# Seven products for the seventh up block, weight sums that are additions and partly accumulating transfers, and down chunks over two blocks

## The chip, the cores and the metric

One core of one Trainium2 chip. The metric is the device time of one execution in microseconds (us), the median of several runs. Everything else that is quoted comes from one profiled execution of the kernel before, so sums are made against that execution's own time.

Engines are named as the profile names them: PE (TensorE) multiplies, PEld is its weight load, DVE (VectorE) and ACT (ScalarE) do elementwise work, POOL (GpSimd) does little in this kernel, and SP (SyncE) issues the loads from memory.

## The reference

Two decoder layers over 256 tokens of width 2048. Each layer has an attention, a cross attention into 256 memory tokens, and an MLP, each behind an RMS norm and added to the residual. All of the change lies in the MLP:

```python
def sq_relu_mlp(h, wup, wdown):
    return jnp.square(jax.nn.relu(h @ wup)) @ wdown

# per layer, with D_MODEL = 2048 and D_FF = 8192
x = x + sq_relu_mlp(rms_norm(x, mlp_norm[i]), mlp_wup[i], mlp_wdown[i])
```

All numbers are float32.

## The kernel before

**Precision.** A weight tile arrives as float32 (`raw`, 128 x 2048, 1 MB) and is split into two float32r tiles: `whi` (a cast, on ACT) and `wlo = raw - whi` (a subtraction, on DVE). Activations are split the same way into a `unit`. A product is then three matmuls: hi x hi, hi x lo, lo x hi.

**Jobs and buffers.** A *job* is one weight tile: one load (issued by SP), and two half splits (`split_pieces`: each half is one ACT cast of 128 x 1024 and one DVE subtraction of the same size). There are six `raw` buffers (`RAWS = 6`), and four buffers each for `whi` and `wlo`, so splits can be two jobs ahead of PE and no more. `fill` issues the loads of jobs ahead of their use. PE runs in program order; the order of the other engines' instructions is chosen by the scheduler when the kernel is built, and each of them is then in order.

**The MLP.** The 8192 hidden columns are cut into eight blocks of 1024, each of two halves of 512. The tokens are two tiles `t` of 128. A plain up block (`Chunk`, kind `"up"`) is eight jobs of 24 matmuls. A `Seven` block computes the same by seven products instead of eight (a Strassen/Winograd scheme over two token tiles, two halves of K, two halves of the columns): products `p1` to `p7`, each as two jobs `x = 0, 1` of 12 matmuls. The activation sums `s1` to `s4` are formed once per layer (`Forms`). The weight sums are made by DVE on the raw tiles before they are split: `p5`, `p7`, `p6` and `p4` each load one more tile, and combine it with the raw tile of an earlier product (line 766, two instructions per job). The products are then combined by DVE into four hidden tiles (line 794, seven instructions per block), which ACT squares after a relu, PE transposes and ACT and DVE split again.

Six of the eight blocks (`SEVEN = (1, 2, 3, 5, 6, 7)`) are done so; blocks 0 and 4 are plain. A down chunk (`Chunk`, kind `"down"`) accumulates 512 of the 2048 output columns over one or one and a half blocks in two PSUM banks, one per token tile, and is then added to the residual by DVE (line 439).

**Order.** `mlp_line` writes the order of a layer's jobs by hand-made costs: `vector` says what a job costs DVE, `tensor` what it costs PE; a `lead` decides whether the next job is taken from the Seven blocks or from the rest (the other up halves and the down chunks).

Most matmuls and casts are recorded on the line of a helper (155 for a matmul, 193 and 194 for the splits), so groups are read by their tile names: `pr` are the products of the Seven blocks, `mm` all other products, `ax` the transposes and the attention's tiles.

Of the kernel before, what the change touches and what calls it, by code (L numbers as in the profile page):

```python
# [17 lines left out]
P = 128  # L18
# [27 lines left out]
def trunk(ctx, tc, x, xT, mem, memT, positions, gcols, gfinal, lam_vecs, consts, W, out):  # L46
# [16 lines left out]
    def nm(s):  # L63
        serial[0] += 1
        return f"{s}_{serial[0]}"
# [81 lines left out]
    def give_back():  # L147
        free_banks[0] += 1

    def mmul(o, stationary, moving, start, stop):  # L150
        n = 1
        for d in moving.shape[1:]:
            n *= d
        clock[0] += max(0.11, n / 2400 + 0.0133)
        return nc.tensor.matmul(o, stationary, moving, start=start, stop=stop)  # L155

    def flip(o, src):
        clock[0] += 0.109
# [209 lines left out]
    class Forms(Stream):  # L368

        def __init__(self, gcol):
            super().__init__(gcol)
            self.raw = [raw_tile().rearrange("p (k t) -> p k t", t=P) for _ in range(NT)]
# [28 lines left out]
        def sums(self):  # L403
            for key in [(t, h) for t in range(NT) for h in range(2)]:
                for task in self.forms[key].tasks:
                    yield task
            for x in range(2):
                a11, a12, a21, a22 = (self.raw[t][:, 8 * h + 4 * x : 8 * h + 4 * x + 4] for t in range(NT) for h in range(2))
                for key, o, p, q, op in (
                    ("s1", a22, a21, a22, ALU.add), ("s3", a21, a11, a21, ALU.subtract),  # L410
                    ("s2", a22, a22, a11, ALU.subtract), ("s4", a12, a12, a22, ALU.subtract),
                ):
                    nc.vector.tensor_tensor(o, p, q, op)
                    self.halves(key, x, o)
                yield T_TURN
# [308 lines left out]
    class Seven:  # L724


        ORDER = ("p1", "p5"), ("p3", "p7", "p6", "p2", "p4")
        A = {"p1": (0, 0), "p2": (0, 1), "p3": "s4", "p4": (1, 1), "p5": "s1", "p6": "s2", "p7": "s3"}

        def __init__(self, l, b):  # L730
            self.l, self.b = l, b
            self.raw = {}
            self.banks = {}

        def fetch(self, i, j, x):
            raw = raw_tile()
            load(raw, W[f"mlp_wup{self.l}"][4 * (2 * self.b + j) + 2 * i + x])
            return raw

        def job(self, p, x):  # L740
            def run():
                r = self.raw
                other = None
                if p == "p1":
                    r["11"] = o = self.fetch(0, 0, x)
                elif p == "p5":
                    o = self.fetch(0, 1, x)
                    other, args = r.pop("11"), lambda a, b: (a, b, ALU.subtract)
                elif p == "p3":
                    r["22"] = o = self.fetch(1, 1, x)  # L750
                elif p == "p7":
                    r["t3"] = o = self.fetch(0, 1, x)
                    other, args = r.pop("22"), lambda a, b: (b, a, ALU.subtract)
                elif p == "p6":
                    r["t2"] = o = self.fetch(0, 0, x)
                    other, args = r.pop("t3"), lambda a, b: (b, a, ALU.add)
                elif p == "p2":
                    r["21"] = o = self.fetch(1, 0, x)
                else:
                    o = r.pop("t2")  # L760
                    other, args = r.pop("21"), lambda a, b: (a, b, ALU.subtract)
                split = split_pieces(o, 4 * CH, 2)
                for h in range(2):
                    if other is not None:
                        half = slice(2 * h * CH, 2 * (h + 1) * CH)
                        nc.vector.tensor_tensor(o[:, half], *args(o[:, half], other[:, half]))  # L766
                    split.next()
                return split.halves

            return run  # L770

        def items(self):
            return [Item(self, (p, x), [self.job(p, x)]) for group in self.ORDER for x in range(2) for p in group]

        def products(self, a, u, copied, out):
            p, x = u
            form = a.form(self.A[p])
            need(form.tasks)
            if x == 0:
                self.banks[p] = bank("pr")  # L780
            o = self.banks[p]
            for h, (hi, lo) in enumerate(take()):
                for k in range(2):
                    kk = 4 * x + 2 * h + k
                    wh, wl = (w[:, k * CH : (k + 1) * CH] for w in (hi, lo))
                    mmul(o, form[:, 0, kk], wh, kk == 0, False)
                    mmul(o, form[:, 0, kk], wl, False, False)
                    mmul(o, form[:, 1, kk], wh, False, kk == 7)
                pump()
            if x == 0:  # L790
                return

            def add(o, p, q, op=ALU.add):
                nc.vector.tensor_tensor(o, p, q, op)

            c, b = copied, self.banks
            if p in ("p1", "p5"):
                c[p] = work.tile([P, CH], F32, tag="ev", name=nm(p), bufs=EVS)
                nc.scalar.copy(c[p], o)
            elif p == "p6":  # L800
                u2, c12 = (work.tile([P, CH], F32, tag="ev", name=nm("u"), bufs=EVS) for _ in range(2))
                add(u2, b["p6"], c["p1"])
                add(c["p5"], u2, c["p5"])
                add(c12, b["p3"], c["p5"])
                out(0, 1, c12)
                add(c["p5"], b["p7"], c["p5"])
                out(1, 1, c["p5"])
                add(u2, b["p7"], u2)
                c["u3"] = u2
            elif p == "p2":  # L810
                add(c["p1"], b["p2"], c["p1"])
                out(0, 0, c["p1"])
            elif p == "p4":
                add(c["u3"], c["u3"], b["p4"], ALU.subtract)
                out(1, 0, c["u3"])

    def mlp_line(l):

# [2 lines left out]
        def up(b, h):  # L821
            return Chunk(l, "up", [(b, h)]).items()

        def down(*halves):
            return [i for c in range(4) for i in Chunk(l, "down", halves, c).items()]

        def both(b):
            return (b, 0), (b, 1)

        line = up(0, 0) + up(0, 1)  # L830
# [12 lines left out]

        def tensor(item):
# [6 lines left out]
        lead, now = 0.0, 0  # L851
        while rest or seven:
            of = rest[0].of if rest else None
            late = rest and of.kind == "down" and any(usable.get(h, math.inf) > now for h in of.halves)
# [5 lines left out]
            if item.of.__class__ is Seven:  # L860
                usable.update({(item.of.b, h): now + 6 for h in range(2)} if item.u == ("p4", 1) else {})
            elif item.of.kind == "up" and item.u == 3:
                usable[item.of.halves[0]] = now + 4
        return line + after, down(*both(7))

    mlp_lines = {l: mlp_line(l) for l in range(2)}

# [193 lines left out]
    def mlp(l, norm, gnext):  # L1061
# [1 line left out]
        rstd = keep2(norm.rstd, 1.0, "r1")  # L1063
        hid = {}

        chunk = {}
        copied = {}

        def out(b, c, t, src, r, wait):
# [31 lines left out]
        def run(line, nxt=None):  # L1101
            for item in line:
                of = item.of
                if isinstance(of, Seven):
                    of.products(
                        a, item.u, copied,
                        lambda t, c, r, b=of.b: out(b, c, t, r, r, T_SQ + 7.0),
                    )
                    continue
                n = len(of.all)  # L1110
# [2 lines left out]
                        finish_chunk(of, matmul_chunk(acts_of(of), turns=True), nxt)  # L1113
                    continue
                if item.u == 0:
                    chunk["ps"] = [bank("mm") for _ in range(NT)]
                    chunk["acts"] = acts_of(of)
                act = chunk["acts"][item.u]
                need(act.tasks)
                for h, (hi, lo) in enumerate(take()):  # L1120
                    for t in range(NT):
                        unit_part(chunk["ps"][t], act, h, hi, lo, t, item.u == 0, item.u == n - 1)
                if item.u == n - 1:
                    finish_chunk(of, chunk["ps"], nxt)

        line, end = mlp_lines[l]
        limit = free_banks[0] - 1
# [274 lines left out]
```

## Time and profile before

| what | value |
|---|---|
| runs, median (lowest to highest of 3) | 2261.57 us (2261.05 to 2264.02) |
| profiled execution, span | 2260.9 us, 0.7 us under the median |
| granted PE clock | 0.999 |
| PE busy | 2236.6 us, 99% of the span |
| DVE busy | 1764.3 us, 78% |
| ACT busy | 1337.3 us, 59% |
| POOL busy | 104.5 us, 5% |
| loads | 475.71 MB, mean 210 GB/s |
| first to last product of the Seven blocks, layer 0 | 545.6 to 1123.4 us |
| the same, layer 1 | 1608.2 to 2185.5 us |

The span runs from the first to the last instruction. Durations of matmuls overlap (one lasts 0.39 us and the next starts 0.227 us after it), so PE counts as busy in gaps of up to 0.16 us. Waits are put down to the event that came last.

### The profile page before, as it was taken

The numbers are of one execution on the slowest core, as the hardware profiler recorded it, in microseconds if no ns is written. First come the engines' busy times: TensorE is split into PE (matmuls) and PEld (weight loads), VectorE is DVE, ScalarE is ACT, GpSimd is POOL, SyncE is SP. The second block draws the span as 40 slices with busy tenths as digits, with TensorE's granted clock in tenths as the row PEclk, the third lists the DMA queues.
The fourth block names the chain that finished last, engine by engine and source line by source line (L and its number), as shares of the span: only waits on it lengthen the run. The fifth ranks groups of instructions, "written<-read, shape, count | busy, mean of one in ns | idle before, by whom it ended". The sixth has DMA issues, their size and how long they took to land.

```text
span 2260.9 us, 27589 instructions
## 1 busy us (share of the span) xinstructions
PE 2236.6 (99%) x10569; PEld 1862.3 (82%) x10569; DVE 1764.3 (78%) x2002; ACT 1337.3 (59%) x1787; POOL 104.5 (5%) x194
## 2 busy tenths in 40 slices
PE   9999999999999999999999999999999999999998
PEld 7888888888888888888889888888888888888886
DVE  6665647778889989888865766778788998888975
ACT  7554546666565665656645655656666656566554
POOL 0201010000000000000000311000000000000001
PEclk9999999999999999999999999999999999999999
DMA  9446555436666667666745334744766676666662
GB/s 362 168 141 214 201 181 208 156 131 235 249 238 227 249 236 259 231 234 223 259 160 184 106 140 149 251 140 149 259 225 241 230 272 222 243 227 246 253 243 75
DMA packets 72564, 475.71 MB, mean 210 GB/s; under 512 B 8304, under 2 KB 8688, under 8 KB 17904
## 3 DMA queue, kind: packets, MB, share of 16 engines
q1 hardware_dynamic: 71856, 472.90, 58.9%
q8 instruction: 83, 1.36, 0.2%
q10 hardware_dynamic: 576, 1.05, 0.2%
q14 instruction: 49, 0.40, 0.1%
HBM read 471.82 MB, written 2.10 MB: 210 GB/s over the span
## 4 chain that ended last, share of the span: by engine, by line
PE 87%; DVE 6%; DMA 4%; issue 1%; ACT 1%; ACTq 0%; DVEq 0%; POOLq 0%
PE mm L155 67%; PE pr L155 14%; DMA raw<-in_mlp_wup_dram 4%; DVE wlo L194 3%; PE ax L155 3%; DVE raw L766 2%; PE ax L159 2%; PE mm L159 1%; ACT whi L193 1%; DMA raw<-in_da_wqkv_dram 0%; DVE x L439 0%; DVE unit L316 0%; DVE unit L488 0%; DVE os L659 0%; DVE unit L289 0%
## 5 line engine op out<-in xcount | busy, mean ns | idle before, releaser
L155 PE MATMUL mm<-whi,unit 128*128 128x512 f32 (+2 forms) x4800 | 1516.4, 389 | 1.3 <-ACT unit L572 0.9
L193 ACT CAST whi<-raw 128x1024 fp32r<-128x1024 f32 (+3 forms) x938 | 976.6, 1041 | 789.4 <-PE mm L155 647.2
L194 DVE TENSOR_TENSOR wlo<-raw,whi 128x1024 fp32r<-128x1024 f32 (+3 forms) x938 | 1124.0, 1211 | 382.8 <-ACT whi L193 366.5
L155 PEld LDWEIGHTS mm<-whi,unit 128*128 128x128 f32 x4800 | 897.8, 188 | 179.0 <-ACT unit L572 1.3
L155 PE MATMUL mm<-wlo,unit 128*128 128x512 f32 (+2 forms) x2400 | 927.7, 387 | 3.9 <-DVE wlo L194 3.7
L155 PEld LDWEIGHTS mm<-wlo,unit 128*128 128x128 f32 x2400 | 451.8, 188 | 90.8 <-DVE wlo L194 7.7
L155 PE MATMUL pr<-whi,unit 128*128 128x512 f32 x1344 | 432.7, 391 | 0.0
L155 PEld LDWEIGHTS pr<-whi,unit 128*128 128x128 f32 x1344 | 252.6, 188 | 51.5
L155 PE MATMUL pr<-wlo,unit 128*128 128x512 f32 x672 | 263.5, 392 | 7.1 <-DVE wlo L194 6.9
L766 DVE TENSOR_TENSOR raw<-raw,raw 128x1024 f32<-128x1024 f32 x192 | 227.7, 1221 | 22.5 <-DMA raw<-in_mlp_wup_dram 22.1
L155 PEld LDWEIGHTS pr<-wlo,unit 128*128 128x128 f32 x672 | 126.3, 188 | 38.1 <-DVE wlo L194 13.0
L439 DVE TENSOR_TENSOR x<-x,mm 128x512 f32<-128x512 f32 x192 | 127.4, 682 | 13.4 <-PE mm L155 12.9
L328 POOL TENSOR_TENSOR rs<-rs,mhalf 128x1 f32<-128x1 f32 (+1 forms) x28 | 23.5, 843 | 1275.2 <-DVE rs L327 1275.2
L288 ACT CAST unit<-ax 128x512 fp32r<-128x512 f32 (+1 forms) x88 | 48.6, 564 | 18.7 <-PE ax L159 16.3
L289 DVE TENSOR_TENSOR unit<-ax,unit 128x512 fp32r<-128x512 f32 (+1 forms) x88 | 57.4, 661 | 2.1 <-ACT unit L288 1.8
L501 ACT ACTIVATE p<-ax,nmax 128x256 f32<-128x256 f32 (+1 forms) x80 | 33.6, 428 | 30.0 <-DVE nmax L499 29.5
L322 ACT ACTIVATE junk<-x 128x512 bf16<-128x512 f32 x56 | 35.1, 627 | 9.4 <-DVE x L439 8.4
L1300 POOL TENSOR_TENSOR x<-x,unit 128x512 f32<-128x512 f32 x6 | 8.9, 1501 | 665.4 <-ACT junk L322 665.4
L155 PE MATMUL ax<-unit,unit 128*128 128x256 f32 (+1 forms) x240 | 37.2, 281 | 0.0
L155 PEld LDWEIGHTS ax<-unit,unit 128*128 128x128 f32 x240 | 34.4, 190 | 2.5
L155 PE MATMUL ax<-raw,unit 128*128 128x256 f32 (+1 forms) x240 | 35.3, 279 | 0.8 <-ACT unit L487 0.6
L155 PEld LDWEIGHTS ax<-raw,unit 128*128 128x128 f32 x240 | 32.0, 191 | 2.4 <-ACT unit L487 1.0
(141 smaller groups left out, 924.4 us busy)
## 6 DMA issues: line engine op xcount, KB each, us to landing
raw<-in_mlp_wup_dram SPq DMA_DIRECT2D x176, 1024.0 KB, 4.9
raw<-in_mlp_wdown_dram SPq DMA_DIRECT2D x128, 1024.0 KB, 5.0
raw<-in_da_wqkv_dram SPq DMA_DIRECT2D x45, 1024.0 KB, 5.1
raw<-in_da_wo_dram SPq DMA_DIRECT2D x16, 1024.0 KB, 5.0
raw<-in_ca_wkv_dram SPq DMA_DIRECT2D x16, 1024.0 KB, 5.0
raw<-in_mla_wo_dram SPq DMA_DIRECT2D x16, 1024.0 KB, 5.2
raw<-in_ca_wq_dram SPq DMA_DIRECT2D x8, 1024.0 KB, 5.0
raw<-in_ca_wo_dram SPq DMA_DIRECT2D x8, 1024.0 KB, 5.0
```

Of the source, the lines that this page charges most:

```text
L155: return nc.tensor.matmul(o, stationary, moving, start=start, stop=stop)
L159: nc.tensor.transpose(o, src, ident)
L193: nc.scalar.copy(hi, r)
L194: nc.vector.tensor_tensor(lo, r, f32(hi), ALU.subtract)
L288: nc.scalar.copy(hi, src)
L289: nc.vector.tensor_tensor(dst[:, 1, :n, t * P : (t + 1) * P], src, f32(hi), ALU.subtract)
L322: nc.scalar.activation(junk[:, : src.shape[1]], src, AF.Square, accum_out=acc)
L328: nc.gpsimd.tensor_tensor(r[:, :n], r[:, :n], mhalf.broadcast_to([P, n]), ALU.pow)
L439: nc.vector.tensor_tensor(xc, xc, ps, ALU.add)
L501: nc.scalar.activation(pr[:, i * w : (i + 1) * w], sb[:, i * w : (i + 1) * w], AF.Exp, bias=nmax[:, i : i + 1], accum_out=ssum[:, i : i + 1],)
L766: nc.vector.tensor_tensor(o[:, half], *args(o[:, half], other[:, half]))
L1300: nc.gpsimd.tensor_tensor(xs[t][:, cc], xs[t][:, cc], gf[:, cc], ALU.mult)
```

## The change

- `SEVEN` gains block 4, so seven blocks go by seven products and block 0 alone is plain.
- The signs of the activation sums are turned (`s1` and `s4`), so that each weight sum is a sum: `p5` uses `p1`'s tile plus one, `p7` uses `p3`'s plus one, `p6` uses `p7`'s plus one, `p4` uses `p6`'s plus one (`SUM`: the product before, the sum's name, the tile that is added).
- A sum whose name is in `ADDED[l]` is no longer made by DVE. After the tile's last half split, POOL issues a transfer that adds the next tile from memory onto the raw tile in place (`accum_op=ALU.add`), and the next product splits that tile. In layer 0 this holds for `t2` (`p7` to `p6`); in layer 1 for `t3`, `t2` and `t4` (`p3` to `p7` to `p6` to `p4`). `t1` stays with DVE in both.
- The products' order is `p1, p5, p2, p3, p7, p6, p4`, both jobs of one product behind each other. `p2` is accumulated onto `p1`'s bank and `p3` onto `p5`'s, after a copy of `p1` and `p5` has been taken, so five DVE instructions combine a block instead of seven.
- A down chunk covers two blocks where it can: its two banks stay open from one block to the next, and there are 18 chunks per layer instead of 28.
- The order's cost of a job no longer counts a sum that a transfer makes, so in layer 1 the jobs of a block stand closer together.

```diff
-SEVEN = (1, 2, 3, 5, 6, 7)
+SEVEN = (1, 2, 3, 4, 5, 6, 7)
+ADDED = ("t2",), ("t3", "t2", "t4")
...
-                    ("s1", a22, a21, a22, ALU.add), ("s3", a21, a11, a21, ALU.subtract),
-                    ("s2", a22, a22, a11, ALU.subtract), ("s4", a12, a12, a22, ALU.subtract),
+                    ("s1", a22, a21, a22, ALU.subtract), ("s3", a21, a11, a21, ALU.subtract),
+                    ("s2", a22, a22, a11, ALU.subtract), ("s4", a12, a12, a22, ALU.add),
...
-        ORDER = ("p1", "p5"), ("p3", "p7", "p6", "p2", "p4")
+        ORDER = "p1", "p5", "p2", "p3", "p7", "p6", "p4"
+        B = {"p1": (0, 0), "p2": (1, 0), "p3": (1, 1)}
+        SUM = {"p5": ("p1", "t1", (0, 1)), "p7": ("p3", "t3", (0, 1)), "p6": ("p7", "t2", (0, 0)), "p4": ("p6", "t4", (1, 0))}
+        AFTER = {before: p for p, (before, _, _) in SUM.items()}
...
+                if p in self.B:
+                    o = self.fetch(*self.B[p], x)
                 else:
-                    o = r.pop("t2")
-                    other, args = r.pop("21"), lambda a, b: (a, b, ALU.subtract)
+                    before, name, block = self.SUM[p]
+                    if name in self.added:
+                        o = self.raw.pop((before, x))
+                    else:
+                        o, other = self.fetch(*block, x), self.raw.pop((before, x))
                 split = split_pieces(o, 4 * CH, 2)
                 for h in range(2):
                     if other is not None:
                         half = slice(2 * h * CH, 2 * (h + 1) * CH)
-                        nc.vector.tensor_tensor(o[:, half], *args(o[:, half], other[:, half]))
+                        nc.vector.tensor_tensor(o[:, half], o[:, half], other[:, half], ALU.add)
                     split.next()
+                if p in self.AFTER:
+                    self.raw[p, x] = o
+                    _, name, block = self.SUM[self.AFTER[p]]
+                    if name in self.added:
+                        add = nc.gpsimd.dma_start(o, self.source(*block, x), accum_op=ALU.add)
+                        tc.keep_in_program_order(add)
...
+            onto = {"p2": "p1", "p3": "p5"}.get(p)
             if x == 0:
-                self.banks[p] = bank("pr")
+                self.banks[p] = self.banks[onto] if onto else bank("pr")
...
-        rest = (
-            up(4, 0) + down(*both(0)) + down(*both(1), (4, 0)) + up(4, 1) + down(*both(2))
-            + down(*both(3), (4, 1)) + down(*both(5)) + down(*both(6))
-        )
+        def down(b):
+            shut, begun = ((0, 1), (2, 3)) if b % 2 else ((2, 3), (0, 1))
+            line = []
+            for c in shut:
+                line += opened.pop(c)[2:] if c in opened else Chunk(l, "down", both(b), c).items()
+            for c in begun:
+                if b == MLP_BLOCKS - 1:
+                    line += Chunk(l, "down", both(b), c).items()
+                else:
+                    opened[c] = Chunk(l, "down", both(b) + both(b + 1), c).items()
+                    line += opened[c][:2]
+            return line
...
-                return 2 + 2 * (p in ("p5", "p7", "p6", "p4")) + x * {"p6": 4, "p2": 2, "p4": 2}.get(p, 0) * 0.55
+                summed = p in Seven.SUM and Seven.SUM[p][1] not in ADDED[l]
+                return 2 + 2 * summed + x * {"p6": 4, "p4": 2, "p2": 1}.get(p, 0) * 0.55
```

The order that `mlp_line` gives in layer 1, with `d` for a down job (24 matmuls): blocks 1 and 2 run `p2x0 p2x1 d p3x0 p3x1 p7x0 p7x1 p6x0 p6x1 d d d p4x0 p4x1`, blocks 3, 4 and 5 `p2x0 p2x1 d p3x0 p3x1 p7x0 p7x1 p6x0 d p6x1 d d p4x0 d p4x1`, blocks 6 and 7 `p2x0 d p2x1 p3x0 p3x1 p7x0 p7x1 d p6x0 p6x1 d d d p4x0 p4x1`. In layer 0 it is, for block 2, `p2x0 p2x1 p3x0 p3x1 p7x0 d p7x1 d p6x0 p6x1 d p4x0 d p4x1`.

DVE in layer 1, block 5, before the change, from the split of `p5`'s second job onward. `raw_15992` is `p3`'s tile, `raw_16016` `p7`'s and `raw_16042` `p6`'s; the sums (L766) stand ahead of splits (L194) of jobs that PE needs earlier:

```order
L766 TENSOR_TENSOR raw_16016<-raw_15992,raw_16016 128x1024 [waits DMAHW7_49,DMAHW0_49,DVE_49]
L766 TENSOR_TENSOR raw_16016<-raw_15992,raw_16016 128x1024
L194 TENSOR_TENSOR wlo_15912<-raw_15903,whi_15911 128x1024 [waits Activation_49]
L194 TENSOR_TENSOR wlo_15950<-raw_15947,whi_15949 128x1024 [waits DMAHW5_49,Activation_49]
L194 TENSOR_TENSOR wlo_15954<-raw_15947,whi_15953 128x1024 [waits Activation_49]
L766 TENSOR_TENSOR raw_16042<-raw_16016,raw_16042 128x1024 [waits DMAHW1_49,DVE_49]
L766 TENSOR_TENSOR raw_16042<-raw_16016,raw_16042 128x1024 [waits DVE_49]
L194 TENSOR_TENSOR wlo_15973<-raw_15970,whi_15972 128x1024 [waits DMAHW6_49,Activation_49]
L194 TENSOR_TENSOR wlo_15977<-raw_15970,whi_15976 128x1024 [waits Activation_49]
L194 TENSOR_TENSOR wlo_15995<-raw_15992,whi_15994 128x1024 [waits Activation_49]
```

The same place after the change (layer 1, block 5, from `p3`'s first job): `raw_16287` is the tile of `x = 0` and `raw_16322` that of `x = 1`, each split in turn as `p3`, `p7` and `p6`:

```order
L195 TENSOR_TENSOR wlo_16290<-raw_16287,whi_16289 128x1024 [waits DMAHW1_49,Activation_49]
L195 TENSOR_TENSOR wlo_16294<-raw_16287,whi_16293 128x1024 [waits Activation_49]
L195 TENSOR_TENSOR wlo_16325<-raw_16322,whi_16324 128x1024 [waits DMAHW2_49,Activation_49]
L195 TENSOR_TENSOR wlo_16329<-raw_16322,whi_16328 128x1024 [waits Activation_49]
L195 TENSOR_TENSOR wlo_16346<-raw_16287,whi_16345 128x1024 [waits DMASW6_49,Activation_49]
L195 TENSOR_TENSOR wlo_16350<-raw_16287,whi_16349 128x1024 [waits Activation_49]
L290 TENSOR_TENSOR unit_16367<-ax_16462,unit_16367 128x4x128 [waits Activation_49]
L195 TENSOR_TENSOR wlo_16371<-raw_16322,whi_16370 128x1024 [waits DMASW7_49,Activation_49]
L195 TENSOR_TENSOR wlo_16375<-raw_16322,whi_16374 128x1024 [waits Activation_49]
L195 TENSOR_TENSOR wlo_16404<-raw_16287,whi_16403 128x1024 [waits DMASW0_49,Activation_49]
L195 TENSOR_TENSOR wlo_16408<-raw_16287,whi_16407 128x1024 [waits Activation_49]
```

The sums are gone from this stretch. Each third and fifth pair of splits waits for an accumulating transfer (`DMASW`) onto the tile that the pair two jobs earlier has read.

POOL in the same block after the change (before it, POOL has nothing in this stretch); each row waits for DVE's last split of the same tile, and the other semaphores name older transfers:

```order
L768 DMA raw_16287<-in_mlp_wup_dram 128x2048 [waits DMAHW1_49,DMAHW3_49,DMAHW0_49,DMAHW6_49,DMASW6_49,DVE_49]
L768 DMA raw_16322<-in_mlp_wup_dram 128x2048 [waits DMAHW2_49,DMAHW4_49,DMASW5_49,DVE_49]
L768 DMA raw_16287<-in_mlp_wup_dram 128x2048 [waits DMASW6_49,DVE_49]
L768 DMA raw_16322<-in_mlp_wup_dram 128x2048 [waits DMASW7_49,DVE_49]
L768 DMA raw_16287<-in_mlp_wup_dram 128x2048 [waits DMASW0_49,DVE_49]
L768 DMA raw_16322<-in_mlp_wup_dram 128x2048 [waits DMASW1_49,DVE_49]
```

Six transfers per block now stand on POOL, in the order `t3`, `t2`, `t4`, each for `x = 0` and then `x = 1`.

More of the change, by code (lines that the diff above doesn't have):

```diff
@@ L154, in mmul @@
         clock[0] += max(0.11, n / 2400 + 0.0133)
-        return nc.tensor.matmul(o, stationary, moving, start=start, stop=stop)
+        return nc.tensor.matmul(o, stationary, moving, start=start, stop=stop, skip_group_check=not alone)
     def flip(o, src):
@@ L853, in mlp_line @@
             of = rest[0].of if rest else None
-            late = rest and of.kind == "down" and any(usable.get(h, math.inf) > now for h in of.halves)
+            late = rest and of.kind == "down" and usable.get(of.halves[rest[0].u], math.inf) > now
             take_seven = seven and (not rest or late or lead <= 0)
@@ L1064, in mlp @@
         hid = {}
-        chunk = {}
         copied = {}
```

94 lines of the change are left out of this document (44 added, 50 removed).

## Prediction

> **What bounds the kernel now.** I read the busy shares first, then the shares of the chain that ended last, then the two MLP stretches apart.
>
> ```profile
> span 2260.9 us, 27589 instructions
> PE 2236.6 (99%) x10569; PEld 1862.3 (82%) x10569; DVE 1764.3 (78%) x2002; ACT 1337.3 (59%) x1787; POOL 104.5 (5%) x194
> PE 87%; DVE 6%; DMA 4%; issue 1%; ACT 1%; ACTq 0%; DVEq 0%; POOLq 0%
> ```
>
> PE is busy nearly throughout, but the chain runs 6% over DVE and 4% over loads, so some of PE's time is waiting that overlapping matmul records hide. To find it I price PE's work from two pieces of the chain without a wait, and hold this against the stretches. The columns after the stretch and its length are the busy time and count of PE, PEld, DVE, ACT and POOL, then clock, DMA share and GB/s; the third row is line 159 alone (PE, PEld), the transposes in layer 0.
>
> ```profile
> 569.93 5.44 PE pr L155 x24
> 641.68 0.44 PE ax L159 x4
> ...
> 545.60:1123.40 577.80, 572.12 (x2561) 469.58 (x2560) 510.66 (x492) 356.52 (x385) 0.00 (x0) 1.00 0.67 239
> 1608.20:2185.50 577.30, 571.97 (x2560) 469.47 (x2559) 510.60 (x492) 356.49 (x385) 0.00 (x0) 1.00 0.68 240
> ...
> 545.60:1123.40 577.80, 16.80 (x112) 13.81 (x112) 1.00 0.67 239
> ```
>
> A matmul takes 5.44 / 24 = 0.2267 us. Layer 0's stretch holds 2561 - 112 = 2449 matmuls, 555.2 us, and 112 / 4 groups of transposes, 12.3 us: 567.5 of 577.8. So 10.3 us are lost there, about 10 in layer 1, 20 together. A piece of the chain shows how (start, length, engine, tile):
>
> ```profile
> 649.00 1.06 ACT whi L193
> 650.09 1.24 DVE wlo L194
> 651.34 4.92 DMA raw<-in_mlp_wup_dram
> 656.34 0.13 DVE raw L766
> 657.49 1.22 DVE raw L766
> 658.70 1.15 DVE wlo L194
> 659.89 1.42 PE pr L155 x5
> ...
> DVE raw L766 <- DMA raw<-in_mlp_wup_dram: 22.1, 27, 2.0
> PEld pr L155 <- DVE wlo L194: 13.0, 14, 1.3
> ```
>
> A weight sum (L766) stands in DVE's order ahead of a split that PE needs sooner, and waits for its own load. DVE so waits 22.1 us in 27 places, and PE's products 13.0 us behind DVE.
>
> **The change, part by part.**
>
> *Matmuls.* A block by products is 14 jobs of 12 matmuls, 168; plain, 8 jobs of 24, 192. One block per layer: 48 fewer, 48 x 0.2267 = 10.9 us less. PE sets the end and nothing covers this, so it is a gain of 10.9.
>
> *DVE and ACT.* The rows:
>
> ```profile
> L193 ACT CAST whi<-raw 128x1024 fp32r<-128x1024 f32 (+3 forms) x938 | 976.6, 1041 | 789.4 <-PE mm L155 647.2
> L194 DVE TENSOR_TENSOR wlo<-raw,whi 128x1024 fp32r<-128x1024 f32 (+3 forms) x938 | 1124.0, 1211 | 382.8 <-ACT whi L193 366.5
> L766 DVE TENSOR_TENSOR raw<-raw,raw 128x1024 f32<-128x1024 f32 x192 | 227.7, 1221 | 22.5 <-DMA raw<-in_mlp_wup_dram 22.1
> L439 DVE TENSOR_TENSOR x<-x,mm 128x512 f32<-128x512 f32 x192 | 127.4, 682 | 13.4 <-PE mm L155 12.9
> L794 DVE TENSOR_TENSOR u<-pr,p 128x512 f32<-128x512 f32 x24 | 16.5, 687 | 0.2
> ```
>
> Sums per layer go from 96 to 84 (layer 0: 7 blocks x 6 x 2) and to 28 (layer 1: 7 x 2 x 2): 12 and 68 times 227.7 / 192 = 1.19 us, 14 and 81 less. Combining takes 7 x 5 = 35 instructions instead of 6 x 7 = 42: 7 x 0.69 = 5 less. Residual adds fall from 56 to 36: 20 x 127.4 / 192 = 13 less. Block 4 has 14 jobs instead of 8, so 12 more half splits: 12 x 1.2 = 14 more on DVE, 12 x 1.04 = 12 more on ACT. DVE gets 18 us lighter in layer 0 and 85 in layer 1. ACT, 357 of 577 us busy, covers its 12. Both engines mostly wait for PE (ACT's idle 789.4 is 647.2 behind `mm`), so this by itself moves the end by nothing.
>
> *The lost 20 us.* They hang on sums ahead of splits, so I scale them with the sums left: 84 / 96 leaves 9.0 of 10.3 in layer 0, 28 / 96 leaves 3 of 10 in layer 1, a gain of 8.4. Fewer instructions on DVE help splits that are merely late, so I take 11 (3 and 8). Bounds: 0, the sums left do the same harm; 20, all goes.
>
> *Banks.* Chunks over two blocks keep four of PE's eight banks open. I find no wait for a bank but this one, and adds become fewer: nothing, and less than 1 us either way.
>
> ```profile
> PEld mm L155 <- DVE x L439: 1.0, 4, 0.3
> ```
>
> *Accumulating transfers.* No row before shows one. POOL is empty in both stretches (0.00 x0 above), so they queue behind nothing there, and the older semaphores that they name belong to loads long landed. They begin when DVE's last split of the tile is done, which PE's buffers time, so they cannot be issued early. ACT's split of the next product waits for their landing; its later splits and casts are queued behind that wait, then DVE's, then PE.
>
> In layer 0 only `p7` to `p6` is so made, with down jobs between; by the order of block 2, at least 9.5 us lie between last split and need. Hidden: 0, up to a transfer of 9.5 us.
>
> In layer 1 the transfers form a chain: `p3` split, transfer, `p7` split, transfer, `p6` split, two jobs (2.7 us each) apart. Splits may be two jobs ahead of PE. Take T = 0 as the end of `p2x1` in blocks 3 to 5. PE's order, with a down job 5.44 and the others 12 matmuls, 2.72, is: d to 5.44, `p3x0` 8.16, `p3x1` 10.88, `p7x0` 13.60, `p7x1` 16.32, then `p6x0`, whose first low half is used at 16.5. A split starts within 0.3 us of PE's freeing the buffer:
>
> ```profile
> 848.11 1.05 ACT L193 CAST whi<-raw 128x1024 fp32r<-128x1024 f32 x1 [0.30 <-PE pr L155]
> ```
>
> The second half of `p3x0` is split by 0.2 + 1.05 + 1.24 = 2.5. With L from issue to landing, `t3` lands at 2.5 + L. A whole split takes 1.05 + 2 x 1.24 = 3.5: `p7x0` is done at 6.0 + L, `t2` lands at 6.0 + 2L, and the first half of `p6x0` (2.3) is ready at 8.3 + 2L. Needed at 16.5: PE waits 2L - 8.2 per block. The same count gives 2L - 5.5 for blocks 1 and 2, which have no down job ahead of `p6x1` (13.7 + 2L against 19.2), and the greater of L - 3.6 and 2L - 10.9 for blocks 6 and 7, which have one ahead of `p6x0`. For L between 4.3 and 7.3 the seven blocks add up to 2(2L - 5.5) + 3(2L - 8.2) + 2(L - 3.6) = 12L - 42.8.
>
> L from the rows:
>
> ```profile
> raw<-in_mlp_wup_dram SPq DMA_DIRECT2D x176, 1024.0 KB, 4.9
> q1 hardware_dynamic: 71856, 472.90, 58.9%
> 1571.00:2261.00 690.00, 675.85 (x3025) 555.16 (x3023) 581.95 (x573) 410.72 (x456) 10.73 (x9) 1.00 0.64 227
> ```
>
> The lower bound is a plain load of the same tile, 4.9: a wait of 16 us. The upper is two loads behind one another, since the transfer takes in two tiles, one from memory and one from the buffer: 9.8, 80 us by the stalls of that length. A 1 MB transfer occupies the 16 DMA engines for 0.589 x 2260.9 x 1.0486 / 472.9 = 2.95 us, so a second pass over the tile adds at least that if it is not overlapped: 4.9 + 2.95 = 7.9. A little of it should overlap, so I take 7.4: 12 x 7.4 - 42.8 = 46 us.
>
> [...]
>
> SP's loads of `p7`, `p6`, `p4` become POOL's in layer 1, so two of the six raw buffers are held from `p3` to `p4`, and the other four carry the rest. A job of 5.44 us still covers a load of 4.9: 0. If that cover goes, PE waits for loads, first at `mm`.
>
> **The sum.** 2260.9 - 10.9 - 11 + 46 = 2285, and 0.7 from span to median: 2286. Its own range: L of 6.0 (29 us) to 8.7 (63 us) gives 2269 to 2303.
>
> **The rivals.**
>
> *Faster: the transfers land like loads.* With L = 4.9 the waits are 16, and with relief of 11 the time is 2256; with the waits gone and the 20 us recovered, 2231. Its middle is 2244. It decides at 12L - 42.8 = 21.9, so L = 5.4. For it: DMA is 0.68 busy in the stretch, so there is room. Against: a second operand must be read.
>
> [...]
>
> *Much slower: the transfers crowd the DMA engines.* Layer 1's last stage moves 152 loads, 152 x 2.95 = 448 of 690 us, 0.65, as the 0.64 above. Now it moves 170, of which 42 count twice: 212 x 2.95 = 625, 0.91. Then L is 9.8 or more, and loads fall late as well: 2260.9 - 21.9 + 80 = 2319. Against: it is still under 1.
>
> *The sums left stand ahead of splits as before,* so that only the waits move: relief 0, 11 us onto each case, 2297 with my L. The transfers do then what the change says, and DVE's lighter load buys nothing. One in five, within the others.
>
> **Chances.** A measurement of this kernel tells about 0.2% (4.5 us) from no change. My forecast 0.42; transfers like loads 0.38; between them, L of 5.0 to 5.8, within 0.2%, 0.07; crowded engines 0.13. So faster 0.38, same 0.07, slower 0.55. The range runs from 2236, which leaves out the best third of the fast case, to 2312, short of the crowded one. The least certain number is L: the rows bound it by a factor of two and its sign turns inside.
>
> **What will show it.** Matmul records of the MLP fall by 48. In layer 1, ACT's `whi` or DVE's `wlo` wait for `raw` from POOL's transfers, some 28 times, and PE's products behind them; POOL's issue rows give L directly. Layer 1's stretch should be some 46 - 8 - 5.4 = 33 us longer than 577.3, layer 0's 3 + 5.4 = 8 shorter than 577.8. If layer 1 is the shorter, L is under 5.4 and my chain is wrong; if PE waits at `mm` for loads, the crowding is right; if DVE's sums still wait 20 us, the relief is.

## The result, and the profile after

The changed kernel takes 2361.62 us (median of 4 runs, 2358.34 to 2365.3) beside 2262.26 of before: a ratio of 1.0441, interval 1.0426 to 1.0455. It is 4.4% slower. The forecast of 2286 had the direction and a quarter of the size, and its range ended at 2312.

The page of the changed kernel, with the parts that answer to those shown of before: span, busy time by engine, shares of the chain that ended last, DMA queues, and loads of one tile with the median time to landing.

```profile
span 2358.1 us, 27600 instructions
PE 2266.0 (96%) x10521; PEld 1872.3 (79%) x10521; DVE 1671.7 (71%) x1892; ACT 1357.4 (58%) x1815; POOL 153.8 (7%) x250
q1 hardware_dynamic: 68976, 451.92, 53.2%
q0 software_dynamic: 8064, 58.72, 13.3%
PE 72%; DMA 12%; DVE 8%; issue 5%; ACT 2%; ACTq 0%; POOLq 0%; DVEq 0%
raw<-in_mlp_wup_dram SPq DMA_DIRECT2D x156, 1024.0 KB, 5.1
raw<-in_mlp_wup_dram POOLq DMA_DIRECT2D x56, 1024.0 KB, 9.4
```

PE issues 48 instructions fewer (10569 to 10521), as forecast, and DVE is 93 us lighter. The chain nevertheless holds 12% of transfers where it held 4%. The 56 accumulating transfers land after 9.4 us, near the upper bound of 9.8 that was taken from two loads. SP's loads still land in 5.1 in the median; those in flight beside the transfers do not, as layer 0 shows below.

The stretches from the first to the last product of the Seven blocks, layer 0 and layer 1 (columns as before: PE, PEld, DVE, ACT, POOL, then granted clock, DMA share, GB/s):

```profile
522.10:1155.90 633.80, 603.98 (x2645) 493.75 (x2645) 512.66 (x487) 381.72 (x416) 12.44 (x14) 0.97 0.77 259
1617.50:2288.40 670.90, 621.81 (x2669) 498.53 (x2668) 457.00 (x432) 379.95 (x417) 36.94 (x42) 0.97 0.84 246
```

The granted clock has fallen from 1.00 to 0.97 in both. To compare kernels whose stretches hold different jobs, I take each PE instruction's distance to the next beyond what it needs (0.227 us for a matmul of 512 columns), and split the sum: "slow" where the matmul itself runs longer than at a granted clock of 1.00 (0.39 us for those 512 columns), "idle" the rest. "Lost" is the sum of the two. Both are in us, for one profiled execution of each kernel, in the stretches of the two layers:

| kernel | span | layer 0: idle + slow | layer 1: idle + slow |
|---|---|---|---|
| before | 2260.9 | 10.3 + 1.3 | 9.9 + 1.3 |
| changed | 2358.1 | 37.5 + 12.5 | 65.2 + 16.4 |
| none: no transfers | 2254.8 | 13.4 + 1.5 | 12.1 + 1.4 |
| plain: transfers that do not add | 2277.8 | 14.4 + 1.9 | 29.8 + 3.9 |
| pin: all DVE sums late | 2395.8 | 60.1 + 22.0 | 63.8 + 21.1 |
| soft3: sums three jobs back | 2337.5 | 29.0 + 4.7 | 59.5 + 16.0 |
| nonesoft3: the same without transfers | 2281.3 | 23.9 + 2.9 | 23.8 + 2.9 |
| t2t4: one sum more by transfer in layer 0 | 2338.4 | 22.1 + 3.4 | 65.2 + 20.4 |
| spaced: layer 1 in another order | 2304.8 | 34.3 + 13.3 | 25.6 + 3.7 |
| warm: PE kept busy in layer 0 | 2380.9 | 32.5 + 4.9 | 64.5 + 25.4 |
| halves: transfers of half a tile | 2331.8 | 35.3 + 9.9 | 49.7 + 9.2 |
| t4only: t4 alone by transfer | 2256.1 | 14.2 + 1.6 | 11.7 + 1.2 |

Lost time rose by 50.0 - 11.6 = 38.4 us in layer 0 and 81.6 - 11.2 = 70.4 in layer 1. With 10.9 saved on matmuls this gives 97.9, against 97.2 measured between the two spans. So the loss is located: 27 us of idle PE in layer 0, 55 in layer 1, and 26 of matmuls at a lower clock.

**Layer 1.** A piece of the chain in block 1 (start, length, what; rows of "issue" left out):

```profile
1663.44 1.06 ACT whi L194
1664.53 1.24 DVE wlo L195
1666.17 8.08 DMA raw<-in_mlp_wup_dram
...
1674.32 1.05 ACT whi L194
1675.40 2.37 DVE wlo L195 x2
1678.17 8.01 DMA raw<-in_mlp_wup_dram
...
1686.27 1.05 ACT whi L194
1687.35 1.24 DVE wlo L195
1688.63 4.23 PE pr L156 x11
```

This is the chain that the prediction drew, step by step: split of `p3`, transfer, split of `p7`, transfer, split of `p6`, and PE behind it. The waits of layer 1's stretch (engine, line, releaser: us, times, longest):

```profile
ACT whi L194 <- DMA raw<-in_mlp_wup_dram: 88.2, 26, 6.0
PEld pr L156 <- ACT whi L194: 39.2, 22, 4.4
PE pr L156 <- ACT whi L194: 29.4, 18, 4.0
```

**Layer 0.** Here the chain piece is another one, in block 2 (rows of "issue" left out):

```profile
654.23 12.53 DMA raw<-in_mlp_wup_dram
666.78 0.04 DVE raw L762
667.93 1.22 DVE raw L762
669.15 1.15 DVE wlo L195
670.34 7.48 PE mm L156 x23
```

Behind the transfer stands DVE's weight sum (L762), not a split of `p6`. It is the sum for `p4`, which reads `p6`'s tile. DVE's order there, where `raw_1114` is `p4`'s tile, `raw_1077` the one that `p7`, the transfer and `p6` use, and `raw_1094` that of the down job ahead of `p6`:

```
L762 TENSOR_TENSOR raw_1114_5705<-raw_1114_5705,raw_1077_5525 128x1024 [waits DMAHW2_49,DMASW2_49]
L762 TENSOR_TENSOR raw_1114_5705<-raw_1114_5705,raw_1077_5525 128x1024
L195 TENSOR_TENSOR wlo_1096_5604<-raw_1094_5601,whi_1095_5603 128x1024 [waits DMAHW0_49,Activation_49]
```

The sum waits for the accumulating transfer (DMASW2), and the split that PE needs next is queued behind it. In layer 0's stretch DVE's sums wait 51.5 us; in the kernel before, both layers together had 22.1:

```profile
DVE raw L762 <- DMA raw<-in_mlp_wup_dram: 51.5, 18, 8.1
PE mm L156 <- DVE wlo L195: 27.1, 8, 5.1
```

Each of the seven blocks has one long wait of such a sum (5.5 to 8.1 us), with a down job's split and then PE behind it. PE's seven waits add up to 27.1 us by the table's measure, which is all of the 27.2 by which layer 0's idle time rose.

What the sum waits for differs. In blocks 2, 3 and 4 it is the transfer. In blocks 1, 5, 6 and 7 the transfer had landed 2.7 to 4.1 us earlier, and the sum waits for its own plain load, which SP had issued between the block's two transfers and which landed 11.3 to 12.2 us later. In block 1 (chain, start and length):

```profile
560.34 11.68 DMA raw<-in_mlp_wup_dram
...
572.13 0.13 DVE raw L762
```

The waits of layer 0's sums behind POOL's transfers and behind SP's loads (us, times), the landing of SP's loads there, and the DMA engines while block 1's two transfers are in flight (columns as before):

```profile
DVE raw L762: 19.8, 3
DVE raw L762: 31.7, 15
DMA to landing us min/median/max: 4.6/5.0/12.2
558.40:574.50 16.10, 13.62 (x62) 10.92 (x61) 8.55 (x9) 8.35 (x9) 1.90 (x2) 1.00 0.97 245
```

The median of SP's loads hides this: in each block one load is issued between the two transfers and lands after 11.1 to 12.2 us, while the 121 loads that overlap with no transfer land after 5.0 (median). While a block's two transfers are in flight the DMA share is 0.89 to 0.97, against 0.77 over the whole stretch. So layer 0 has both: a sum that stands ahead of an earlier job's split, and DMA engines that are nearly full just then.

**The clock.** PE's matmuls around that wait (start, length, tile, idle time ahead):

```profile
664.81 0.39 PE L156 MATMUL mm<-whi,unit 128*128 128x512 f32 x1
670.34 0.79 PE L156 MATMUL mm<-wlo,unit 128*128 128x512 f32 x1 [5.14 <-DVE wlo L195]
670.93 1.06 PE L156 MATMUL mm<-whi,unit 128*128 128x512 f32 x2
671.78 0.63 PE L156 MATMUL mm<-wlo,unit 128*128 128x512 f32 x1
```

A matmul of 0.39 us takes 0.79 and 0.63 behind the gap. Each of layer 0's seven waits of 2.75 to 5.3 us (by the table's measure) is followed by 7 to 14 slow matmuls; in layer 1 one of 2.5 us was, too. The granted clock was 1.00 from 664.0 to 667.5 us, 0.50 from 668.0 to 674.4, and 1.00 again from 674.7 to 676.0. In the kernel before, the longest wait from layer 0's MLP on was 1.4 us, and no matmul there took over 0.51 us.

### The profile page after: what moved, and what is told of

It is laid out like the page before. It is cut to its first block, busy times and chain, and to the rows that moved or that the text cites. A ratio compares the mean times of both kernels' runs of the same rounds, so it can differ in the third digit from the quotient of the medians.

```text
span 2358.1 us, 27600 instructions
## 1 busy us (share of the span) xinstructions
PE 2266.0 (96%) x10521; PEld 1872.3 (79%) x10521; DVE 1671.7 (71%) x1892; ACT 1357.4 (58%) x1815; POOL 153.8 (7%) x250
## 3 DMA queue, kind: packets, MB, share of 16 engines
q0 software_dynamic: 8064, 58.72, 13.3%
## 4 chain that ended last, share of the span: by engine, by line
PE 72%; DMA 12%; DVE 8%; issue 5%; ACT 2%; ACTq 0%; POOLq 0%; DVEq 0%
PE mm L156 56%; DMA raw<-in_mlp_wup_dram 11%; PE pr L156 11%; DVE wlo L195 5%; PE ax L156 3%; PE ax L160 2%; DVE raw L762 2%; ACT whi L194 2%; PE mm L160 1%; DMA raw<-in_mlp_wdown_dram 0%; DVE unit L386 0%; DMA raw<-in_da_wqkv_dram 0%; DVE x L439 0%; DVE raw L413 0%; DVE unit L317 0%
## 5 line engine op out<-in xcount | busy, mean ns | idle before, releaser
L195 DVE TENSOR_TENSOR wlo<-raw,whi 128x1024 fp32r<-128x1024 f32 (+2 forms) x962 | 1148.3, 1212 | 527.0 <-ACT whi L194 512.4
L194 ACT CAST whi<-raw 128x1024 fp32r<-128x1024 f32 (+2 forms) x962 | 995.9, 1041 | 845.5 <-PE mm L156 619.8
L156 PE MATMUL mm<-whi,unit 128*128 128x512 f32 (+3 forms) x4544 | 1444.1, 391 | 1.5 <-ACT unit L572 0.9
L156 PEld LDWEIGHTS mm<-whi,unit 128*128 128x128 f32 x4544 | 855.9, 189 | 170.4 <-ACT unit L316 1.5
L156 PE MATMUL mm<-wlo,unit 128*128 128x512 f32 (+3 forms) x2272 | 883.8, 389 | 27.9 <-DVE wlo L195 27.8
L156 PE MATMUL pr<-whi,unit 128*128 128x512 f32 x1568 | 523.5, 402 | 29.6 <-ACT whi L194 29.4
L156 PEld LDWEIGHTS pr<-whi,unit 128*128 128x128 f32 x1568 | 302.7, 193 | 100.5 <-ACT whi L194 39.2
L156 PE MATMUL pr<-wlo,unit 128*128 128x512 f32 x784 | 316.6, 404 | 21.4 <-DVE wlo L195 21.0
L762 DVE TENSOR_TENSOR raw<-raw,raw 128x1024 f32<-128x1024 f32 x112 | 132.1, 1221 | 61.4 <-DMA raw<-in_mlp_wup_dram 60.7
L768 POOL DMA_DIRECT2D raw<-in_mlp_wup_dram x56 | 49.4, 882 | 1213.5 <-DVE wlo L195 696.9
L290 DVE TENSOR_TENSOR unit<-ax,unit 128x512 fp32r<-128x512 f32 (+1 forms) x88 | 57.4, 661 | 10.9 <-ACT unit L289 9.9
L156 PE MATMUL ax<-raw,unit 128*128 128x256 f32 (+1 forms) x240 | 35.4, 280 | 0.8 <-ACT unit L487 0.6
```

The source lines that it names most:

```text
L194: nc.scalar.copy(hi, r)
L195: nc.vector.tensor_tensor(lo, r, f32(hi), ALU.subtract)
L290: nc.vector.tensor_tensor(dst[:, 1, :n, t * P : (t + 1) * P], src, f32(hi), ALU.subtract)
L762: nc.vector.tensor_tensor(o[:, half], o[:, half], other[:, half], ALU.add)
L768: add = nc.gpsimd.dma_start(o, self.source(*block, x), accum_op=ALU.add)
```

## The experiments

All spans are in the table above; each kernel is the changed one with the edit shown. Where no interval is given, the kernel ran once.

**No transfers (none).**

```diff
-ADDED = ("t2",), ("t3", "t2", "t4")
+ADDED = (), ()
```

> No accumulating transfers in either layer (ADDED empty): DVE makes all four sums, everything else of the change stays, and the job order is layer 0's in both layers. Theory A (the transfers make the whole loss): PE waits only for sums that stand ahead of splits, as before, 20 us x 112/96 sums = 23.5 us; 2260.9 - 10.9 + 3.5 = 2253, faster than before by 0.2 to 0.6%. Rival B (another part does harm as well: banks open over two blocks, p2 and p3 on p1's and p5's banks, the new product order): 2290 or more, with PE waiting at pr or mm for DVE's adds.

Measured: span 2254.8; over 10 runs 2259.01 beside 2260.93, ratio 0.9988, interval 0.9978 to 0.9997, a little less than A's 0.2%. A holds with one addition: the transfers, with the order that their cost rule gives, make the whole loss. The edit changes the order of jobs in layer 0 as well, which the expectation overlooked (block 2 now ends `p6x0 d p6x1 d d p4x0 p4x1`); the next run keeps the order. Banks, products in place and the new order of products do no harm that shows. The DMA share of layer 0 is 0.76 here and was 0.67 before: the kernel before made `p4`'s sum of two tiles that it already had, so the change loads 18 tiles more per layer, 12 of them for `p4`. Against before, 10.9 us of matmuls are saved and 28.4 - 22.8 = 5.6 are lost again on waits, which leaves 5.3; the spans differ by 6.1.

**Transfers that do not add (plain).** `p7`, `p6` and `p4` then multiply an overwritten tile instead of a sum.

```diff
-add = nc.gpsimd.dma_start(o, self.source(*block, x), accum_op=ALU.add)
+add = nc.gpsimd.dma_start(o, self.source(*block, x))
```

> The same POOL transfers without the addition (they overwrite the tile, so the products of p7, p6 and p4 are not the reference's); order and waits unchanged. Theory A (the addition, a second read, makes the 9.4 us): issue to landing 4.9 to 5.5 us, 2.9 us of engine time each; layer 1's stretch loses 15 to 25 us instead of 82, layer 0's 12 to 20 instead of 50; time 2255 to 2275. Rival B (POOL's queue is slow whatever it carries): issue to landing 8 us or more, time 2330 or more.

```profile
q0 software_dynamic: 8064, 58.72, 7.2%
raw<-in_mlp_wup_dram POOLq DMA_DIRECT2D x56, 1024.0 KB, 5.3
```

With the same queue, bytes and order of jobs, a transfer lands in 5.3 us instead of 9.4. On the 16 engines a transfer occupies 0.072 x 2277.8 / 56 = 2.93 us, with the addition 0.133 x 2358.1 / 56 = 5.60: 1.91 times. So it is the addition, not POOL's queue, and not the order of jobs alone: layer 0 loses 16.3 us here and 50.0 with the addition. The span is 2.8 us over A's range, and layer 1 loses 33.7, over A's 15 to 25. Its transfers land in 5.2 us (median of 42), and it still idles 29.8, against 12 x 5.2 - 42.8 = 20 by the prediction's chain plus 3 left of sums.

**All DVE sums pinned (pin).**

```diff
-nc.vector.tensor_tensor(o[:, half], o[:, half], other[:, half], ALU.add)
+tc.keep_in_program_order(nc.vector.tensor_tensor(o[:, half], o[:, half], other[:, half], ALU.add))
```

> Each sum that DVE still makes is pinned behind the DVE instructions that the program writes ahead of it, so no sum stands ahead of an earlier job's split; the transfers stay. Theory A (layer 0's loss is DVE's sum for p4, which waits for the transfer onto p6's tile with an earlier job's splits behind it): layer 0's lost time falls from 50 us to 15 or less, layer 1's by under 10; time 2315 to 2330. Rival B (layer 0 loses because the transfer itself is late for p6's own split): lost time in layer 0 stays at 35 to 50; time 2345 or more.

Both theories missed: layer 0 lost 82 us. The pinned sums stood behind all DVE work written earlier, and were late for their own splits (ACT's casts wait for them; us, times, longest):

```profile
ACT whi L194 <- DVE raw L762: 183.5, 86, 3.6
```

So this run says nothing about the question, which the next three put again.

**Sums three jobs back, with and without transfers (soft3, nonesoft3).**

```diff
 split = split_pieces(o, 4 * CH, 2)
+behind = lows[-5].ins
...
+sum_ = nc.vector.tensor_tensor(o[:, half], o[:, half], other[:, half], ALU.add)
+tc.add_manual_dep(sum_.ins, behind.name, mybir.DependencyInfo(mybir.DependencyClass.NoSync, mybir.DependencyReason.DATA), reason="order")
```

`lows` lists the `wlo` splits as the program writes them, so `lows[-5]` is the last one of the job three before. nonesoft3 has `ADDED = (), ()` besides.

> The changed kernel, with each DVE sum ordered behind the last split of the job three before its own, and nothing else pinned (pin put the sums behind all DVE work written earlier, which made them late themselves). In layer 0 the sum for p4 now stands behind p6's split of the same x, which needs the same transfer anyway. Theory A (layer 0 loses because that sum waits for the transfer with a down job's splits behind it): layer 0's lost time falls from 50 us to 18 or less, layer 1's stays within 10 of 82; time 2315 to 2330. Rival B (the transfer itself comes too late for p6's split): layer 0 still loses 35 or more, time 2345 or more.

> No transfers, and each DVE sum behind the last split of the job three before its own. Theory A (what is left of lost time without transfers, 13.4 + 12.1 us, is DVE's sums that wait for their load ahead of splits): lost time falls to 5 to 8 us per layer, time 2240 to 2247, 0.6 to 0.9% faster than before. Rival B (DVE has too much to do just behind p7 and p6, so a later sum makes its own split late): lost time 12 or more per layer, 2253 or more.

soft3 came out between: layer 0 lost 33.7 us, not 50, nor 18, and just under B's 35. nonesoft3 shows that the ordering has a price of its own: where no transfer is about, 26.8 us are lost in layer 0 instead of 14.9 (2284.05 beside 2263.14 of the kernel before, ratio 1.0095, 1.0078 to 1.0112), since sums now come late for their own splits, as its rival B said. So 50.0 falls to 33.7 although the ordering costs something. How much of the 33.7 is the transfer's own lateness these two do not tell, since nonesoft3 also has the order of jobs of the kernel without transfers.

**No sum left on `p6`'s tile in layer 0 (t2t4).** Order and layer 1 unchanged.

```diff
-ADDED = ("t2",), ("t3", "t2", "t4")
+ADDED = ("t2", "t4"), ("t3", "t2", "t4")
+COSTED = ("t2",), ("t3", "t2", "t4")
...
-summed = p in Seven.SUM and Seven.SUM[p][1] not in ADDED[l]
+summed = p in Seven.SUM and Seven.SUM[p][1] not in COSTED[l]
```

> Layer 0 with transfers for t2 and t4, job order and layer 1 unchanged: DVE has no sum left that reads p6's tile, so nothing of DVE waits for a transfer except p6's and p4's own splits. Theory A: layer 0 loses 25 us or less, time 2335 or less, although it has 14 transfers more. Rival B (every added transfer costs layer 0 its wait, 26 + 11 us per 14 transfers): layer 0 loses 65 us or more, time 2375 or more.

Layer 0 loses 25.5 us instead of 50.0, half a microsecond over A's limit, with 28 transfers instead of 14; the span is 2338.4, 3 over. Rival B (65 or more) is out. So at least 24.5 us of layer 0's loss hang on the sum for `p4`, in the same order of jobs. The edit takes away the sum, its place ahead of the down job's split and its plain load together, so it does not tell the wait for the transfer from the wait for the slowed load. The 25.5 that stay are 9.2 more than where the transfers do not add (16.3); ACT's casts wait 126.0 us for transfers over both layers, of which layer 1, in the same order, had 88.2 in the changed kernel. That leaves some 38 for layer 0, an estimate, so part of the 9.2 is the transfers' own lateness.

**Layer 1 with work between (spaced).** Two down jobs behind `p3`, `p7` and `p6` each, one behind `p1` and `p5`.

```diff
-take_seven = seven and (not rest or late or lead <= 0)
+take_seven = seven and (not rest or late or (owed <= 0 if l else lead <= 0))
...
+owed = owed - 1 if not take_seven else {"p1": 1, "p5": 1, "p3": 2, "p7": 2, "p6": 2}.get(item.u[0], 0) * item.u[1]
```

> Layer 1 only: two down jobs (10.9 us) stand between p3 and p7, p7 and p6, p6 and p4, one after p1 and one after p5; the transfers stay. Theory A (layer 1 loses because the chain p3, transfer, p7, transfer, p6 has no work between): with 9.4 us a transfer, p7's first half is ready 14.2 us after p2x0's end and needed at 19.0; layer 1's lost time falls from 82 us to 15 or less, time 2285 to 2300. Rival B (transfers crowd the DMA engines, whatever the order): landing rises over 10 us or loads come late, layer 1 still loses 45 or more, time 2320 or more.

```profile
1616.00:2229.10 613.10, 595.37 (x2640) 482.19 (x2640) 454.34 (x429) 378.47 (x414) 36.94 (x42) 1.00 0.88 267
raw<-in_mlp_wup_dram POOLq DMA_DIRECT2D x56, 1024.0 KB, 10.3
```

With the same 42 transfers in layer 1, landing even later there (10.3 us, as over all 56) and at a DMA share of 0.88, layer 1 loses 29.3 us instead of 81.6, and the clock is back at 1.00. So about two thirds of the 81.6 were the missing work between. It is not 15, and the span is 4.8 us over A's range. In one piece of its chain, behind `p4` and `p1`, DVE's sum for `p5` waits 4.6 us for its load; no down job stands there now.

**Half tiles (halves).**

```diff
-add = nc.gpsimd.dma_start(o, self.source(*block, x), accum_op=ALU.add)
+for h in range(2):
+    half = slice(2 * h * CH, 2 * (h + 1) * CH)
+    add = nc.gpsimd.dma_start(o[:, half], self.source(*block, x)[:, half], accum_op=ALU.add)
```

> The changed kernel, with each accumulating transfer made as two of half the tile (1024 of 2048 columns), so that each half waits for the DVE split of its half alone and the next product's first half can be split when its half has landed. Theory A (layer 1 pays for the latency of a chain of two transfers per block): if a half lands in 5 to 6 us, the chain to p6's first half is 1.2 + 5.5 + 2.3 + 5.5 + 2.3 = 17 us instead of 25, against the 16.5 that are there; layer 1's lost time falls from 82 us to 20 to 45, and the time to 2290 to 2325. Rival B (the price is one per transfer, not by bytes, or the DMA engines are full): a half takes 8 us or more, layer 1 loses 75 us or more, time 2350 or more.

Between the two: a half lands in 7.9 us (median of layer 1; 5.4 at best), not 5 to 6, and layer 1 loses 58.9, not 45 or 75. Half the bytes do not cost half the latency where two halves follow each other. It confirms only that a shorter chain loses less.

**PE kept busy (warm).** 64 small matmuls that add exact zeros, ahead of the job behind `p7x1`, in layer 0.

```diff
+stuff = l == 0 and before == ("p7", 1)
+before = item.u
...
+if stuff:
+    for _ in range(64):
+        nc.tensor.matmul(of.ps[0][:64, :64], identr[:, :64], identr[:, 64:], start=False, stop=False, skip_group_check=True)
```

> The changed kernel, with 64 matmuls of 64 x 64 that add exact zeros ahead of the down (or up) job behind p7's second job, in layer 0 alone: PE has them to do in the place where it idles 3 to 5 us per block. Theory A (the clock falls because PE idled, so PE's wait is charged twice, 11 us in layer 0): time lost to slow matmuls in layer 0's stretch falls from 12.5 us to 6 or less, and the time by 4 to 10 us, 2348 to 2354. Rival B (the clock falls for another reason, such as traffic): 12.5 stays, and the time is the same or up to 10 us longer by the extra matmuls.

Slow matmuls in layer 0 fell from 12.5 to 4.9 us, as A said, but the time, which A had falling, rose by 23. The filler did not go into idle time (32.5 us of that are left): PE's waits moved from the down jobs to the products behind them, where nothing fills them: those of `mm` for DVE's splits fell from 27.8 to 2.7 us, and those of `pr` rose from 21.0 to 41.5. Layer 1, whose order was not edited, lost 8 us more than in the changed kernel. So the run does not isolate the clock's price.

**t4 alone, in the order of the kernel without transfers (t4only).**

```diff
-ADDED = ("t2",), ("t3", "t2", "t4")
+ADDED = ("t4",), ("t4",)
+COSTED = (), ()
...
-summed = p in Seven.SUM and Seven.SUM[p][1] not in ADDED[l]
+summed = p in Seven.SUM and Seven.SUM[p][1] not in COSTED[l]
```

> Only t4 (p6 to p4) by accumulating transfers, in both layers, in the job order of the kernel without transfers. Without transfers, the sums for p4 make 14.9 of DVE's 24.7 us of waiting for loads, ahead of splits; here they are gone, and p4's transfer has two to four jobs with down jobs between (16 us needed, 24 to 27 there). Theory A (a transfer that has this much work ahead of its use costs nothing): lost time falls from 14.9 and 13.5 us to 6 to 11 per layer, time 2243 to 2251. Rival B (any accumulating transfer makes loads and splits late by its 5.6 us on the DMA engines): lost time 20 us or more per layer, 2262 or more.

```profile
raw<-in_mlp_wup_dram POOLq DMA_DIRECT2D x28, 1024.0 KB, 11.7
522.60:1121.10 598.50, 590.06 (x2645) 484.00 (x2644) 541.94 (x515) 380.69 (x416) 0.00 (x0) 1.00 0.76 274
523.00:1122.60 599.60, 590.29 (x2644) 483.75 (x2643) 510.85 (x486) 381.18 (x416) 12.44 (x14) 1.00 0.80 274
```

The second row is the kernel without transfers, the third this one, both layer 0. The transfers take 11.7 us, against 9.4 in the changed kernel, and cost nothing on balance: 15.8 and 12.9 us lost against 14.9 and 13.5. B is out. But A missed as well: lost time did not fall to 6 to 11, and nothing is won. The sums for `p4` no longer wait, since they are gone, and the others wait 28.1 us for loads, where all of them together waited 23.7 in the kernel without transfers (both by the rows of waits). It runs in 2257.77 beside 2262.36, ratio 0.9980, interval 0.9971 to 0.9989: the best of the kernels here, and not to be told from the one without transfers (0.9988).

## Why the prediction was wrong

It had the direction, the matmuls (48 fewer) and the chain in layer 1. Its sum was 2285; the profiled execution took 73 us more. Four terms were off; the first is a step that failed, the third a term that the sum left out, the other two are sizes.

*"Hidden: 0" for layer 0's transfers.* This step failed: 30 us more idle time than forecast (37.5 against 10.3 - 3 = 7.3). The prediction asked only when `p6`'s split needs the tile. It did not ask who else reads it: DVE's sum for `p4` does, and stands ahead of a down job's split. Nor did it ask which loads are in flight beside the transfers: in four of the seven blocks that sum waits for its own plain load, which took 11.3 to 12.2 us. The prediction had described the early sum for plain loads, and its own profile rows showed it. The bound failed too: it allowed 9.5 us, and layer 0's transfers take longer (the first row; the second is layer 1):

```profile
DMA to landing us min/median/max: 9.6/11.3/12.9
DMA to landing us min/median/max: 7.8/8.2/12.4
```

Why they take longer in layer 0, at a lower mean DMA share (0.77 against 0.84), was not tried. What the traces show is that in layer 0 a block's two transfers and a plain load are in flight together, with 2 x 5.60 + 2.95 = 14 us of engine time in 16 to 18, while in layer 1 each transfer mostly overlaps only with the ends of the ones before and behind it.

*The size of L.* Taken as 7.4; layer 1 measured 8.2. Above 7.3 the longer of the two stalls of blocks 6 and 7 is 2L - 10.9, so the seven blocks add up to 14L - 57.4: 57 us at 8.2 instead of 46 (and 64, not 63, at the 8.7 of the prediction's range). With 3 left of sums this is 60, against 65.2 of idle time. So the mechanism stands, 11 us are L and 5 are not accounted for. The slope fits as well: from the transfers that do not add (5.2) to those that do (8.2), in the same order, layer 1's idle time rises by 35.4, 11.8 per us of L.

*A wait priced once.* The prediction added up how long PE waits and nothing for what follows. Slow matmuls cost 12.5 + 16.4 - 2.6 = 26 us more than before, over a third of the miss. Behind the 5.3 us wait of block 2 in the changed kernel a matmul took 0.79 us instead of 0.39, at a granted clock of 0.50. How long a wait has to be for this was not tried. The price is not fixed: the changed kernel, t2t4 and warm have the same order written for layer 1 and idle 64.5 to 65.2 us in it, yet lose 16.4, 20.4 and 25.4 to slow matmuls. What sets this was not tried.

*The relief of 11 us.* It was scaled with the number of sums left. t4only has a quarter fewer sums than the kernel without transfers and loses the same 28.7 us against 28.4: the wait goes to the next sum. So the step "They hang on sums ahead of splits, so I scale them with the sums left" has the place right and the scaling wrong.

Of the rivals, the crowded DMA engines came nearest in time (2319). For layer 1, where they were priced, they are wrong: L was 8.2 and not 9.8, and spaced recovered 52 us there at a higher DMA share. In layer 0, for which the rival had no term, loads do fall late, and PE waits at `mm` behind them, the sign that the prediction had named. That the sums left stand ahead of splits as before was right, and worse than priced, since they now wait for transfers and loads of 11 to 12 us.

## What to carry to other kernels

When a load turns into something slower, list every reader of the tile on every engine, in that engine's order, not only the one that the change is made for: here an early reader of another job held up DVE, and PE behind it. Look at the loads in flight beside the slow transfers one by one, since their median of 5.0 us showed nothing of the 11.1 to 12.2. A transfer that adds belongs where its whole latency has other work beside it: with that it cost nothing on balance even at 11.7 us (t4only), while in a chain of two without it a microsecond of latency cost 11.8 us over seven blocks (from 5.2 to 8.2 us, layer 1). And add to a PE wait the slow matmuls behind it: in layer 0 seven waits of 2.75 to 5.3 us, 27.1 us together, brought 11 us of them.

## What was not expected of the hardware

An accumulating transfer of 1 MB holds the DMA engines for 5.60 us against 2.93 for the same transfer without the addition, and lands after 9.4 against 5.3 (changed kernel and plain, medians of 56). A plain load issued between two of them landed after 11.1 to 12.2 us instead of 5.0 (changed kernel, layer 0). Halving the transfer brought layer 1's median only from 8.2 to 7.9 us. On POOL, issuing one took 0.88 us with the addition and 0.54 without:

```profile
L768 POOL DMA_DIRECT2D raw<-in_mlp_wup_dram x56: 863/876/1037, 558.4 to 2263.7; - x56
L768 POOL DMA_DIRECT2D raw<-in_mlp_wup_dram x56: 540/540/737, 559.5 to 2183.3; - x56
```

The first row is the changed kernel, the second the one that does not add (shortest, median and longest in ns).
